# silu(c) times w_ada: one half of the rows summed on VectorE, the result turned in 32x32 blocks

## The chip, the cores and the metric

The kernel runs on one core of one Trainium2 chip. The metric is the device time of one execution in microseconds (us), the median over the runs shown. The engines are named as in the profile: PE is TensorE (PEld its weight loads), DVE is VectorE, ACT is ScalarE, POOL is GpSimd, SP is SyncE, which here only issues DMAs.

## What is computed

A decoder layer on x (512 tokens of 2048 features). Only its opening matters here:

```python
mod = silu(c) @ w_ada[l] + b_ada[l]
shift, scale, gate = split(mod, 3, axis=-1)
h = rmsnorm(x, ln_g[l]) * (1.0 + scale[:, None]) + shift[:, None]
p = h @ w_in[l] + b_in[l]
...
```

`silu(c) @ w_ada` is a product of one row of 2048 numbers with a 2048 x 6144 matrix. Its first 4096 columns (shift and scale) are needed before h exists. After p come a matrix-memory group and a sparse-attention group, an output projection, a gate, the residual and a last RMSNorm.

## The kernel before, in words

All products on float32 data are made of three single passes: an operand is split into hi + lo (`split`, line 119: ACT casts the hi half at line 123, then DVE or POOL subtracts for the lo half at line 126, as the pattern `pat` says), and PE adds hi·hi, hi·lo and lo·hi into the same PSUM bank.

The opening stage (lines 129 to 236) works on 16 k-tiles of 128 features.

- Lines 134 to 136 load the packed columns and x as four tiles xs of 128 tokens. Lines 150 to 158 take the row norms: two squares on ACT (L153), two small DVE steps (L155, L156), a power on POOL (L157), one scaling on DVE (L158).
- Lines 176 to 185 transpose x on PE (L180) into 16 tiles xt of 128 features x 512 tokens, copied out of PSUM by DVE and ACT in turn (L185, L183).
- `modulate(k)` (line 190) loads one tile of weights kow (448 KB) and, in `gemv`, the four ada tiles of this k-tile (4 x 512 KB, line 167). `gemv` multiplies them with cb, which is silu(c) repeated over 32 columns: 16 matmuls of 256 columns, four at a time in the four column groups of PE (L169), which leave four partial sums in the PSUM tile gp_s. DVE copies them out (L173), and two matmuls with one column each (L195, L196; the column sel holds ones at the four partial sums) add them and turn the result so that features lie on partitions. DVE makes the shift and the factor md from them (L198 to L200), then hf = xt·factor + shift (L202); ACT casts hf to hhi (L205); DVE subtracts for hlo (L206).
- `first_tiles(k)` (line 211) splits kow and issues 21 matmuls of 512 columns into seven PSUM tiles ko: seven of hhi with the hi half (L218), seven of hlo with the hi half (L220), seven of hhi with the lo half (L221).

The loop at line 226 calls `modulate(k + 1)` ahead of `first_tiles(k)`. The order on each engine is then chosen by the framework's scheduler; `tc.issue_after` holds an instruction behind another. Buffers that bound the overlap: eight ada tiles (two k-tiles), three kow tiles, four hi and four lo halves (two k-tiles), one PSUM bank "o" for gp_s. All DMAs go through SP in one queue. After the stage, `proj` (line 238) does the same three-pass product for the other column tiles of w_in.

Of the kernel before, what the change touches and what calls it, by code (L numbers as in the profile page):

```python
# [86 lines left out]
def layer_kernel(ctx: ExitStack, tc: tile.TileContext, x, cols, ada, ada_g, w_ko, w_tiles,  # L87
# [71 lines left out]

    lastdma = [None]  # L160

    def gemv(step, name):
        """silu(c) @ 256 columns of w_ada: four partial sums, one per quadrant of rows"""
        gpb = psb("o", f"gp_{name}")
        for kk in range(4):
            raw = ada_tile(f"ada{name}_{kk}")
            lastdma[0] = nc.sync.dma_start(raw, ada[step, kk]).ins
            for j in range(4):
                pe.matmul(gpb[32 * j:32 * j + 32, 0:256], cb[:, 4 * kk + j, :],  # L169
                          raw[:, j * 256:(j + 1) * 256], start=(kk == 0), stop=(kk == 3),  # L170
                          tile_position=(0, 32 * j))
        gv = st.tile([P, 256], F32, tag="gv", name=f"gv{name}", bufs=2)
        ve.tensor_copy(gv, gpb[:, 0:256])  # L173
        return gpb, gv

    xt = []
    for k in range(KT):
        tp = psb(("pj", "pj", "sc", "sc", "tp", "tp", "ms", "o")[k % 8], f"xt{k}")
        for i in range(NT):
            pe.transpose(tp[:, i * P:(i + 1) * P], xs[i][:, k * P:(k + 1) * P], ident)  # L180
        xt.append(hp.tile([P, T], F32, name=f"xts{k}", tag=f"hlo{k}"))
        if k % 2:
            sc.copy(xt[k], tp)  # L183
        else:
            ve.tensor_copy(xt[k], tp)  # L185
    hhi, hlo = [], []
# [3 lines left out]
    def modulate(k):  # L190
        """h^T of 128 features as hi + lo"""
        raw = raw_tile(f"kow{k}")
        nc.sync.dma_start(raw[:, :KO], w_ko[k * P:(k + 1) * P, :])
        gpb, gv = gemv(k, f"s{k}")
        pe.matmul(gpb[:, 256:257], gv[:, 0:128], col("sel"), start=True, stop=True)  # L195
        last = pe.matmul(gpb[:, 257:258], gv[:, 128:256], col("sel"), start=True, stop=True)  # L196
        md = st.tile([P, 2], F32, name=f"md{k}", tag="md", bufs=2)
        ve.tensor_add(md[:, 0:1], gpb[:, 256:257], col("b_shift", k))  # L198
        ve.tensor_scalar(md[:, 1:2], gpb[:, 257:258], col("b_scale", k), 1.0, op0=ALU.add, op1=ALU.add)
        ve.tensor_mul(md[:, 1:2], md[:, 1:2], col("ln_g", k))  # L200
        hf = st.tile([P, T], F32, name=f"hf{k}", tag="hf", bufs=2)
        ve.tensor_scalar(hf, xt[k], md[:, 1:2], md[:, 0:1], op0=ALU.mult, op1=ALU.add)  # L202
        hh = hp.tile([P, T], F32R, tag=f"hhi{k}", name=f"hhi{k}")
        hl = hp.tile([P, T], F32R, tag=f"hlo{k}", name=f"hlo{k}")
        sc.copy(hh, hf)  # L205
        ve.tensor_sub(hl, hf, hh.bitcast(F32))  # L206
        hhi.append(hh)
        hlo.append(hl)
        return raw, last.ins

    def first_tiles(k, raw, after):
        """the products of one k-tile; those beyond the first few are issued behind `after`"""
        for j0, nj in ((0, 4), (4, 3)):
            wh, wl = split(raw[:, j0 * P:(j0 + nj) * P], nj * P, f"ko{k}_{j0}")
            for j in range(nj):
                ps = ko_ps[j0 + j]
                c = slice(j * P, (j + 1) * P)
                pe.matmul(ps, wh[:, c], hhi[k], start=(k == 0), stop=False)  # L218
                with tc.issue_after(after) if after is not None and j0 + j >= JSEL else nullcontext():
                    pe.matmul(ps, wh[:, c], hlo[k], start=False, stop=False)  # L220
                    pe.matmul(ps, wl[:, c], hhi[k], start=False, stop=(k == KT - 1))  # L221
# [68 lines left out]
    def q_evac(ps, name):  # L290
        """the stacks [hi; lo] and [lo; hi] of the two heads in a tile"""
# [11 lines left out]
    # gate logits (input gates, forget gates, branch gates) as rows  # L303
# [57 lines left out]
    # gaps between tiles of tokens: gp_[h, j, i] = sum of the totals of tiles j .. i-1  # L361
# [14 lines left out]
    # tokens paired by parity on the partitions, with the position term of either block half  # L376
# [21 lines left out]
    def compress(kv):  # L398
        """keys and values of the compressed blocks"""
# [60 lines left out]
    def attend(g, qs, kh, kl, vt):  # L460
# [6 lines left out]
        for i in reversed(range(NT)):  # L467
# [522 lines left out]
```

## Time and profile before

| | us |
|---|---|
| median of 3 runs | 1149.93 (1147.37 to 1151.27) |
| span of the profiled execution, first to last instruction | 1147.1 |
| PE busy in it | 1120.0 |
| DVE busy | 646.4 |
| ACT busy | 531.3 |
| POOL busy | 198.3 |

The profiled execution is one more execution. Its span is 2.8 us below the median of the timed runs and 0.3 us below the lowest of them; what lies around the span is not listed apart. In the profile's rows a matmul's duration contains its pipeline, so two matmuls of one line can overlap; how often a new one starts is read from the start times. A row "x32" covers 32 instructions, from the first start to the last end. One float32 `pe.matmul` gives two records, one for each of two passes.

### The profile page before, as it was taken

The page shows a single profiled execution, that of the slowest core. Times are in us where ns is not written, and L with a number is a line of the kernel's source. Part 1 is how long each engine was busy: PE and PEld are TensorE (multiplying, and loading weights), DVE is VectorE, ACT ScalarE, POOL GpSimd, SP SyncE. Part 2 cuts the span into 40 slices and gives each one's busy share as a digit, 9 for nine tenths or more (in the row PEclk, how much of TensorE's full clock was granted, in tenths as well). Part 3 has the DMA queues.
Part 4 walks back from the last instruction along what each step waited for, and adds up shares of the span by engine and source line. Part 5 has one row for each costly group of instructions (what it writes and reads, how often), then busy time and mean ns, then how long its engine had stood idle before and what let it go on. Part 6 is the DMA issues. An engine that isn't in the chain of part 4 may idle for free.

```text
span 1147.1 us, 16515 instructions
## 1 busy us (share of the span) xinstructions
PE 1120.0 (98%) x5924; PEld 919.0 (80%) x5924; DVE 646.4 (56%) x1649; ACT 531.3 (46%) x1206; POOL 198.3 (17%) x174
## 2 busy tenths in 40 slices
PE   5999999999999999999999999999999999999997
PEld 4677788888888788788788778888888888888896
DVE  5444446205566656775757785668667357344273
ACT  5222253226667657756666743433433354233242
POOL 0000110333235324333533220000000001000000
PEclk9999999999999999999999999999999999999998
DMA  9999432332122122112211353238526332544334
GB/s 371 400 344 351 183 111 90 122 94 91 55 62 68 56 58 73 54 58 64 66 56 56 121 175 92 74 129 279 162 74 198 84 89 73 163 138 125 105 121 156
DMA packets 49330, 150.17 MB, mean 131 GB/s; under 512 B 5856, under 2 KB 7776, under 8 KB 48736
## 3 DMA queue, kind: packets, MB, share of 16 engines
q1 hardware_dynamic: 49248, 149.12, 39.7%
q8 instruction: 46, 0.75, 0.3%
q14 instruction: 36, 0.29, 0.1%
HBM read 144.90 MB, written 4.19 MB: 130 GB/s over the span
## 4 chain that ended last, share of the span: by engine, by line
PE 94%; DVE 3%; DMA 2%; issue 1%; ACT 1%; SPq 0%; ACTq 0%; POOLq 0%; DVEq 0%
PE po L860 4%; PE po L861 4%; PE po L862 4%; PE gp_s L169 3%; PE pj_q L250 3%; PE pj_mz L250 3%; PE pj_mx L250 3%; PE pj_mz L251 3%; PE pj_q L251 3%; PE pj_mz L252 3%; PE pj_mv L250 3%; PE pj_q L252 3%; PE pj_mx L251 3%; PE pj_mv L252 3%; PE pj_mx L252 3%; PE pj_mv L251 3%
## 5 line engine op out<-in xcount | busy, mean ns | idle before, releaser
L485 ACT ACTIVATE ep<-ep,nm 128x512 f32<-128x512 f32 (+3 forms) x128 | 71.2, 557 | 19.4 <-DVE nm L478 18.7
L710 POOL TENSOR_TENSOR sm<-sm,mhalf 128x1 f32<-128x1 f32 x16 | 10.1, 638 | 253.8 <-DVE sm L709 112.5
L749 DVE SCALAR_TENSOR_TENSOR gacc<-adag,sil,gacc 128x512 f32<-128x512 f32 x60 | 48.5, 809 | 8.9 <-DMA adag<-in_dram 8.2
L478 DVE CUSTOM_DVE_ANT_0 ep<-ss,bias 128x512 f32<-128x512 f32 (+3 forms) x64 | 30.3, 486 | 30.7 <-PE tps L504 22.1
L123 ACT CAST ko_0h<-kow 128x512 fp32r<-128x512 f32 x16 | 9.9, 620 | 76.0 <-PE ko L220 76.0
L478 DVE CUSTOM_DVE_ANT_0 ep<-sw,bias 128x512 f32<-128x512 f32 (+3 forms) x64 | 29.9, 486 | 18.9 <-PE sw L546 12.9
L498 DVE TENSOR_SCALAR ep<-ep,ff 128x512 f32<-128x512 f32 (+3 forms) x80 | 33.2, 463 | 0.6
L822 POOL TENSOR_TENSOR rf<-rf,mhalf 128x1 f32<-128x1 f32 x4 | 2.2, 547 | 178.8 <-ACT tz L815 163.1
L508 DVE TENSOR_TENSOR pls<-tps,phs 128x512 fp32r<-128x512 f32 x40 | 27.1, 685 | 10.5 <-ACT phs L507 10.1
L169 PE MATMUL gp_s<-adas,cb 128*32 128x256 f32 x512 | 31.2, 382 | 0.4 <-PE gp_s L196 0.4
L508 DVE TENSOR_TENSOR plw<-tpw,phw 128x512 fp32r<-128x512 f32 x40 | 27.3, 685 | 6.7 <-ACT phw L507 6.0
L465 POOL TENSOR_SCALAR bias<-ct 128x640 f32<-128x640 f32 x16 | 29.4, 1838 | 2.3 <-DVE nm L478 1.2
L507 ACT CAST phw<-tpw 128x512 fp32r<-128x512 f32 x40 | 22.8, 582 | 13.3 <-PE tpw L504 8.4
L485 ACT ACTIVATE ec<-ec,nm 128x32 f32<-128x32 f32 x64 | 20.3, 317 | 17.6 <-DVE nm L478 17.2
L507 ACT CAST phs<-tps 128x512 fp32r<-128x512 f32 x40 | 23.0, 581 | 11.2 <-DVE nm L478 5.0
L504 PE MATMUL tpw<-ct,ep 128*128 128x128 f32 x160 | 26.6, 272 | 0.1
L220 PE MATMUL ko<-hlo,ko_0h 128*128 128x512 f32 x64 | 26.4, 412 | 0.0
L169 PEld LDWEIGHTS gp_s<-adas,cb 128*32 128x32 f32 x512 | 15.1, 110 | 13.8 <-PE ko L220 4.9
L496 ACT ACTIVATE ep<-ep,ff 128x512 f32<-128x512 f32 (+3 forms) x48 | 23.5, 552 | 4.4 <-DVE ff L490 4.3
L478 DVE CUSTOM_DVE_ANT_0 ec<-ss,bias 128x32 f32<-128x32 f32 x48 | 9.0, 188 | 29.1 <-PE ss L536 28.8
L221 PE MATMUL ko<-hhi,ko_0l 128*128 128x512 f32 x64 | 24.9, 390 | 0.0
L504 PE MATMUL tps<-ct,ep 128*128 128x128 f32 x160 | 24.9, 272 | 0.0
(1082 smaller groups left out, 3824.0 us busy)
## 6 DMA issues: line engine op xcount, KB each, us to landing
adas<-in_dram SPq DMA_DIRECT2D x64, 512.0 KB, 7.5
adag<-in_dram SPq DMA_DIRECT2D x64, 256.0 KB, 3.8
wo<-in_dram SPq DMA_DIRECT2D x32, 512.0 KB, 3.6
w_q<-in_dram SPq DMA_DIRECT2D x16, 512.0 KB, 3.7
w_mx<-in_dram SPq DMA_DIRECT2D x16, 512.0 KB, 3.6
w_mv<-in_dram SPq DMA_DIRECT2D x16, 512.0 KB, 3.7
w_mz<-in_dram SPq DMA_DIRECT2D x16, 512.0 KB, 3.6
w_mo<-in_dram SPq DMA_DIRECT2D x16, 512.0 KB, 3.7
```

The source lines that it names most:

```text
L169: pe.matmul(gpb[32 * j:32 * j + 32, 0:256], cb[:, 4 * kk + j, :], raw[:, j * 256:(j + 1) * 256], start=(kk == 0), stop=(kk == 3), tile_pos ...
L250: pe.matmul(ps, wh[:, c], hhi[k], start=(k == 0), stop=False)
L251: pe.matmul(ps, wh[:, c], hlo[k], start=False, stop=False)
L252: pe.matmul(ps, wl[:, c], hhi[k], start=False, stop=(k == KT - 1))
L478: ve.tensor_tensor_reduce(dst, src, bs, -0.125, 3.0e38, ALU.add, ALU.min, nm[:, c:c + 1])
L485: sc.activation(tiles[hd], tiles[hd], AF.Exp, bias=nm[:, 4 * br + hd:4 * br + hd + 1], scale=-1.0, accum_out=zz[:, 4 * br + hd:4 * br + hd ...
L504: pe.transpose(tp[0:rows, hd * P:(hd + 1) * P], srcs[hd], ident)
L508: ve.tensor_sub(pl[0:rows, :], tp[0:rows, :], ph[0:rows, :].bitcast(F32))
L749: ve.scalar_tensor_tensor(acc, raw, w, acc, op0=ALU.mult, op1=ALU.add)
L860: pe.matmul(pss[i][:, :cn], yh[k][:, t], wh[:, c], start=f0, stop=False)
L861: pe.matmul(pss[i][:, :cn], yh[k][:, t], wl[:, c], start=False, stop=False)
L862: pe.matmul(pss[i][:, :cn], yl[k][:, t], wh[:, c], start=False, stop=l0)
```

## The change

Within the opening stage:

- `gemv` takes the four ada tiles of a k-tile in the order 2, 3, 0, 1. The first two are multiplied on PE, now with 64 instead of 256 columns per matmul: each of the four column groups takes its own 32 columns of shift and of scale (8 rows x 4 groups, 64 records). The other two are summed on DVE into acc: one multiplication and seven multiply-adds of 128x256. A ninth round of four matmuls with a tile of ones adds acc into the same PSUM tile.
- The copy gv and the sel matmuls go. One DVE transpose in 32x32 blocks turns the PSUM tile, and md comes from two DVE instructions instead of three (bs1 = b_scale + 1 is made once).
- ACT makes hhi from xt, factor and shift directly, beside DVE's hf, and no longer from hf.
- Both lo halves of kow are made on POOL in the whole stage (`pat[0] = "p"`).
- `first_tiles` goes over the seven tiles three times: hhi with hi, hhi with lo, hlo with hi; the third round is issued behind the ones matmuls of the next k-tile.
- All loads of the stage are chained in program order: x, ada 0, kow 0, ada 1, kow 1, and so on. One of the two squares of each x tile is made on DVE, the scaling is done in two halves, and seven transposes of x stand ahead of the first product, nine behind.

```diff
     for i in range(NT):
-        nc.sync.dma_start(xs[i], x[i * P:(i + 1) * P, :])
+        lastdma[0] = nc.sync.dma_start(xs[i], x[i * P:(i + 1) * P, :]).ins
+    ones = const.tile([P, P], F32, name="ones")
+    gp.memset(ones, 1.0)
...
-    cb = st.tile([P, KT, 32], F32, name="cb")
-    ve.tensor_copy(cb, sil.unsqueeze(2).to_broadcast([P, KT, 32]))
+    cb = st.tile([P, KT // 2, 32], F32, name="cb")
+    ve.tensor_copy(cb, sil[:, KT // 2:].unsqueeze(2).to_broadcast([P, KT // 2, 32]))
+    bs1 = st.tile([P, KT], F32, name="bs1")
+    ve.tensor_scalar_add(bs1, col("b_scale", 0, KT), 1.0)
...
-        for hf in range(2):
-            junk = ada_tile(f"junk{i}{hf}")
-            sc.activation(junk, xs[i][:, hf * 1024:(hf + 1) * 1024], AF.Square,
-                          accum_out=ss[:, 2 * i + hf:2 * i + hf + 1])
+        junk = [ada_tile(f"junk{i}{hf}") for hf in range(2)]
+        sc.activation(junk[0], xs[i][:, 0:1024], AF.Square, accum_out=ss[:, 2 * i:2 * i + 1])
+        ve.tensor_tensor_reduce(junk[1], xs[i][:, 1024:], xs[i][:, 1024:], 1.0, 0.0, ALU.mult, ALU.add,
+                                ss[:, 2 * i + 1:2 * i + 2])
...
-        ve.tensor_scalar_mul(xs[i], xs[i], rr[:, i:i + 1])
+        for hf in range(2):
+            xh = xs[i][:, hf * 1024:(hf + 1) * 1024]
+            ve.tensor_scalar_mul(xh, xh, rr[:, i:i + 1])
+
+    def load_ada(k):
+        raws = []
+        for kk in (2, 3, 0, 1):
+            raw = ada_tile(f"ada{k}_{kk}")
+            with tc.issue_after(lastdma[0]):
+                lastdma[0] = nc.sync.dma_start(raw, ada[k, kk]).ins
+            raws.append(raw)
+        raw = raw_tile(f"kow{k}")
...
+    def gemv(k, raws):
+        acc = st.tile([P, 256], F32, tag="acc", name=f"acc{k}", bufs=2)
+        for r in range(8):
+            w = raws[2 + r // 4][:, (r % 4) * 256:(r % 4 + 1) * 256]
+            if r == 0:
+                ve.tensor_scalar_mul(acc, w, sil[:, r:r + 1])
+            else:
+                ve.scalar_tensor_tensor(acc, w, sil[:, r:r + 1], acc, op0=ALU.mult, op1=ALU.add)
+        gpb = psb("o", f"gp{k}")
+        for r in range(9):
+            w = acc if r == 8 else raws[r // 4][:, (r % 4) * 256:(r % 4 + 1) * 256]
+            w = w.rearrange("p (s c) -> p s c", s=2)
+            for g in range(4):
+                c = slice(32 * g, 32 * g + 32)
+                last = pe.matmul(gpb[c, 0:64].rearrange("p (s c) -> p s c", s=2), ones[:, 0:32] if r == 8 else cb[:, r, :],
+                          w[:, :, c], start=(r == 0), stop=(r == 8), tile_position=(0, 32 * g))
+        tr = st.tile([P, 64], F32, tag="tr", name=f"tr{k}", bufs=2)
+        ve.transpose(tr, gpb[:, 0:64])
+        md = st.tile([P, 2], F32, name=f"md{k}", tag="md", bufs=2)
+        ve.tensor_add(md[:, 0:1], tr[:, 0:1], col("b_shift", k))
+        ve.tensor_scalar(md[:, 1:2], tr[:, 32:33], bs1[:, k:k + 1], col("ln_g", k), op0=ALU.add, op1=ALU.mult)
+        return md, last.ins
...
+    def modulate(k, md):
         hf = st.tile([P, T], F32, name=f"hf{k}", tag="hf", bufs=2)
-        ve.tensor_scalar(hf, xt[k], md[:, 1:2], md[:, 0:1], op0=ALU.mult, op1=ALU.add)
...
-        sc.copy(hh, hf)
+        sc.activation(hh, xt[k], AF.Identity, scale=md[:, 1:2], bias=md[:, 0:1])
+        ve.tensor_scalar(hf, xt[k], md[:, 1:2], md[:, 0:1], op0=ALU.mult, op1=ALU.add)
         ve.tensor_sub(hl, hf, hh.bitcast(F32))
...
+        w = [split(raw[:, j0 * P:(j0 + nj) * P], nj * P, f"ko{k}_{j0}") for j0, nj in ((0, 4), (4, 3))]
+        for p in range(3):
+            for j in range(NKO):
+                wh, wl = w[j // 4]
+                c = slice(j % 4 * P, (j % 4 + 1) * P)
+                with tc.issue_after(after) if p == 2 and after is not None else nullcontext():
+                    pe.matmul(ko_ps[j], (wl if p == 1 else wh)[:, c], (hlo if p == 2 else hhi)[k],
+                              start=(k == 0 and p == 0), stop=(k == KT - 1 and p == 2))
+
+    pat[0] = "p"
```

Where the change moves instructions, the order on three engines is this. The names end in a buffer number; the digit ahead of it is the k-tile.

PE, before, from the product of k-tile 7 on (gp_s7 is its PSUM tile, ko0 to ko6 the first column tiles):

```order
L169 MATMUL gp_s7_703<-adas7_3_722,cb_82 32x256 x4
L218 MATMUL ko0_232<-hhi6_668,ko6_0h_742 128x512
L220 MATMUL ko0_232<-hlo6_669,ko6_0h_742 128x512
L221 MATMUL ko0_232<-hhi6_668,ko6_0l_743 128x512
L218 MATMUL ko4_236<-hhi6_668,ko6_4h_758 128x512
L195 MATMUL gp_s7_703<-ct_67,gvs7_728 128x1
L196 MATMUL gp_s7_703<-ct_67,gvs7_728 128x1
L220 MATMUL ko2_234<-hlo6_669,ko6_0h_742 128x512
```

The same place in the changed kernel:

```order
L195 MATMUL gp7_910<-ada7_2_856,cb_86 32x64 x16
L195 MATMUL gp7_910<-ada7_3_858,cb_86 32x64 x16
L248 MATMUL ko0_317<-hhi6_896,ko6_0h_962 128x512
L248 MATMUL ko6_323<-hhi6_896,ko6_4l_967 128x512
L195 MATMUL gp7_910<-acc7_901,ones_80 32x64 x4
L248 MATMUL ko0_317<-hlo6_897,ko6_0h_962 128x512
L248 MATMUL ko6_323<-hlo6_897,ko6_4h_966 128x512
L195 MATMUL gp8_1006<-ada8_2_952,cb_86 32x64 x16
```

Only the first and the last matmul of a round on ko stand here. Ahead of the ones matmuls there are 14 matmuls on ko, behind them seven, and then the next product begins.

DVE, before, from the copy of the partial sums of k-tile 4 on (ko5_0l and ko5_4l are lo halves of kow 5):

```order
L173 COPY gvs4_518<-gp_s4_493 128x256
L198 TENSOR_TENSOR md4_522<-gp_s4_493,ct_67 128x1
L199 TENSOR_SCALAR md4_522<-gp_s4_493,ct_67 128x1
L200 TENSOR_TENSOR md4_522<-md4_522,ct_67 128x1
L202 TENSOR_SCALAR hf4_526<-xts4_153,md4_522 128x512
L126 TENSOR_TENSOR ko5_0l_673<-kow5_561,ko5_0h_672 128x512
L206 TENSOR_TENSOR hlo4_529<-hf4_526,hhi4_528 128x512
L126 TENSOR_TENSOR ko5_4l_689<-kow5_561,ko5_4h_688 128x384
```

DVE in the changed kernel, from the transpose of k-tile 5 to that of k-tile 6:

```order
L199 STREAM_TRANSPOSE tr5_755<-gp5_718 128x64
L201 TENSOR_TENSOR md5_757<-tr5_755,ct_67 128x1
L202 TENSOR_SCALAR md5_757<-tr5_755,bs1_88,ct_67 128x1
L213 TENSOR_SCALAR hf5_799<-xts5_188,md5_757 128x512
L214 TENSOR_TENSOR hlo5_801<-hf5_799,hhi5_800 128x512
L186 TENSOR_SCALAR acc6_805<-ada6_0_764,sil_84 128x256
L188 SCALAR_TENSOR_TENSOR acc6_805<-ada6_0_764,sil_84,acc6_805 128x256 x3
L188 SCALAR_TENSOR_TENSOR acc6_805<-ada6_1_766,sil_84,acc6_805 128x256 x4
L199 STREAM_TRANSPOSE tr6_851<-gp6_814 128x64
```

The two lo halves left DVE, and the eight instructions on acc stand between the hlo of one k-tile and the transpose of the next. From k-tile 4 on every step reads like this.

POOL, before, after the four powers of the row norms (rst and zt belong to the attention group):

```order
L157 TENSOR_TENSOR rr_87<-rr_87,mhalf_84 128x1 x4
L336 MEMSET rst_1534 4x512
L344 MEMSET zt_1541 64x512
```

POOL in the changed kernel, two of the 16 k-tiles that follow the powers:

```order
L126 TENSOR_TENSOR ko5_0l_867<-kow5_672,ko5_0h_866 128x512
L126 TENSOR_TENSOR ko5_4l_871<-kow5_672,ko5_4h_870 128x384
L126 TENSOR_TENSOR ko6_0l_963<-kow6_768,ko6_0h_962 128x512
L126 TENSOR_TENSOR ko6_4l_967<-kow6_768,ko6_4h_966 128x384
```

In the stage POOL was empty behind the powers; now it has two subtractions for each k-tile.

## Rows read from the trace of the kernel before

**Rows 1.** The page: busy time of PE, and the chain that ended last.
```profile
PE 1120.0 (98%) x5924; PEld 919.0 (80%) x5924; DVE 646.4 (56%) x1649; ACT 531.3 (46%) x1206; POOL 198.3 (17%) x174
...
PE 94%; DVE 3%; DMA 2%; issue 1%; ACT 1%; SPq 0%; ACTq 0%; POOLq 0%; DVEq 0%
```

**Rows 2.** Busy time by stretch: PE, PEld, DVE, ACT, POOL, clock, DMA share, GB/s.
```profile
20.00:40.00 20.00, 18.48 (x171) 13.19 (x169) 10.57 (x24) 5.55 (x11) 0.00 (x0) 1.00 1.03 408
60.00:120.00 60.00, 60.00 (x465) 43.33 (x464) 25.90 (x64) 13.23 (x24) 0.00 (x0) 1.00 0.96 350
```

**Rows 3.** Timeline, PE: one step of the stage, and step 15 (start, length).
```profile
57.25 1.93 PE L169 MATMUL gp_s<-adas,cb 128*32 128x256 f32 x32
...
60.83 0.39 PE L221 MATMUL ko<-hhi,ko_0l 128*128 128x512 f32 x1
61.06 0.84 PE L218 MATMUL ko<-hhi,ko_4h 128*128 128x512 f32 x3
...
61.74 0.28 PE L195 MATMUL gp_s<-ct,gvs 128*128 128x1 f32 x2
...
130.25 1.93 PE L169 MATMUL gp_s<-adas,cb 128*32 128x256 f32 x32
```

**Rows 4.** Timeline, PE: the first 25 ns of one product.
```profile
57.25 0.42 PE L169 MATMUL gp_s<-adas,cb 128*32 128x256 f32 x4
```

**Rows 5.** Timeline, DVE: the start, one step, and the last step of the stage.
```profile
17.26 1.28 DVE L158 TENSOR_SCALAR xs<-xs,rr 128x2048 f32<-128x2048 f32 x1
...
19.99 4.87 DVE L185 COPY xts<-xt 128x512 f32<-128x512 f32 x8
...
26.63 0.16 DVE L198 TENSOR_TENSOR md<-gp_s,ct 128x1 f32<-128x1 f32 x1 [0.70 <-PE gp_s L196]
...
62.28 0.16 DVE L198 TENSOR_TENSOR md<-gp_s,ct 128x1 f32<-128x1 f32 x1 [2.60 <-PE gp_s L196]
...
62.79 0.55 DVE L202 TENSOR_SCALAR hf<-xts,md 128x512 f32<-128x512 f32 x1
...
64.38 0.68 DVE L206 TENSOR_TENSOR hlo<-hf,hhi 128x512 fp32r<-128x512 f32 x1
...
135.28 0.16 DVE L198 TENSOR_TENSOR md<-gp_s,ct 128x1 f32<-128x1 f32 x1 [2.60 <-PE gp_s L196]
```

**Rows 6.** Groups by line and shape: busy, mean ns of one.
```profile
L169 PEld LDWEIGHTS gp_s<-adas,cb 128*32 128x32 f32 x512 | 15.1, 110 | 13.8 <-PE ko L220 4.9 <-PE gp_s L196 0.5 <-issue 0.4
...
L205 ACT CAST hhi<-hf 128x512 fp32r<-128x512 f32 x16 | 9.8, 615 | 3.9 <-DVE hf L202 3.9
L173 DVE COPY gvs<-gp_s 128x256 f32<-128x256 f32 x16 | 6.8, 425 | 16.7 <-PE gp_s L169 16.7
L498 DVE TENSOR_SCALAR ep<-ep,ff 128x256 f32<-128x256 f32 x20 | 6.0, 350 | 0.2
L388 DVE SCALAR_TENSOR_TENSOR cst<-pj_vc,ct 64x256 f32<-64x256 f32 x16 | 7.1, 480 | 6.3 <-PE pj_vc L252 6.2
```

**Rows 7.** Timeline, DVE: two chained multiply-adds on one accumulator.
```profile
764.00 1.54 DVE L589 SCALAR_TENSOR_TENSOR acc<-xp,ct,acc 128x512 f32<-128x512 f32 x2
```

**Rows 8.** One line's instructions: ns shortest/median/longest.
```profile
L749 DVE SCALAR_TENSOR_TENSOR gacc<-adag,sil,gacc x60: 731/748/1855, 649.0 to 891.6; 128x512 f32<-128x512 f32 x60
...
L126 POOL TENSOR_TENSOR w_k_00l<-w_k,w_k_00h x4: 1288/1292/1297, 205.5 to 388.1; 128x512 fp32r<-128x512 f32 x4
```

**Rows 9.** Timeline, DVE and POOL: two places where they meet in SBUF.
```profile
494.17 0.75 DVE L589 SCALAR_TENSOR_TENSOR acc<-xp,ct,acc 128x512 f32<-128x512 f32 x1
...
494.34 1.73 POOL L126 TENSOR_TENSOR w_mv_00l<-w_mv,w_mv_00h 128x512 fp32r<-128x512 f32 x1 [3.01 <-ACT w_mv_00h L123]
...
595.40 1.29 POOL L126 TENSOR_TENSOR w_mz_00l<-w_mz,w_mz_00h 128x512 fp32r<-128x512 f32 x1 [0.24 <-ACT w_mz_00h L123]
...
595.48 1.76 DVE L589 SCALAR_TENSOR_TENSOR acc<-xp,ct,acc 128x512 f32<-128x512 f32 x1
```

**Rows 10.** DMA issues of the first 140 us: size, median us to landing.
```profile
adas<-in_dram SPq DMA_DIRECT2D x64, 512.0 KB, 7.5
kow<-in_dram SPq DMA_DIRECT2D x16, 448.0 KB, 6.1
```

More of the change, by code (lines that the diff above doesn't have):

```diff
@@ L134, in layer_kernel @@
     nc.sync.dma_start(ct[:, :NEARLY], cols[:, :NEARLY])
+    lastdma = [None]
     for i in range(NT):
-        nc.sync.dma_start(xs[i], x[i * P:(i + 1) * P, :])
+        lastdma[0] = nc.sync.dma_start(xs[i], x[i * P:(i + 1) * P, :]).ins
+    ones = const.tile([P, P], F32, name="ones")
+    gp.memset(ones, 1.0)
+    mhalf = const.tile([P, 4], F32, name="mhalf")
+    gp.memset(mhalf, -0.5)
     sil = const.tile([P, KT], F32, name="sil")
     sc.activation(sil, col("c", 0, 16), AF.Silu)
-    cb = st.tile([P, KT, 32], F32, name="cb")
-    ve.tensor_copy(cb, sil.unsqueeze(2).to_broadcast([P, KT, 32]))
-    mhalf = const.tile([P, 4], F32, name="mhalf")
-    gp.memset(mhalf, -0.5)
+    cb = st.tile([P, KT // 2, 32], F32, name="cb")
+    ve.tensor_copy(cb, sil[:, KT // 2:].unsqueeze(2).to_broadcast([P, KT // 2, 32]))
+    bs1 = st.tile([P, KT], F32, name="bs1")
+    ve.tensor_scalar_add(bs1, col("b_scale", 0, KT), 1.0)
     ss = st.tile([P, 2 * NT], F32, name="ss")
@@ L157, in layer_kernel @@
         gp.tensor_tensor(rr[:, i:i + 1], rr[:, i:i + 1], mhalf[:, 0:1], op=ALU.pow)
-        ve.tensor_scalar_mul(xs[i], xs[i], rr[:, i:i + 1])
[L160 to L185, printed above, removed]
-    hhi, hlo = [], []
-    ko_names = list(TILES)[:NKO]
-    ko_ps = [psb(t, f"ko{i}") for i, t in enumerate(("pj", "pj", "sc", "sc", "tp", "tp", "ms"))]
@@ L190, in modulate @@
[L190 to L200, printed above, removed]
+        for hf in range(2):
+            xh = xs[i][:, hf * 1024:(hf + 1) * 1024]
+            ve.tensor_scalar_mul(xh, xh, rr[:, i:i + 1])
@@ new lines, in load_ada @@
+    def load_ada(k):
[6 more added lines that the diff above has]
+        raw = raw_tile(f"kow{k}")
+        with tc.issue_after(lastdma[0]):
+            lastdma[0] = nc.sync.dma_start(raw[:, :KO], w_ko[k * P:(k + 1) * P, :]).ins
+        return raws, raw
+    def gemv(k, raws):
[20 more added lines that the diff above has]
+        return md, last.ins
@@ L208, in modulate @@
         hlo.append(hl)
-        return raw, last.ins
-    def first_tiles(k, raw, after):
[L213 to L221, printed above, removed]
@@ L223, in layer_kernel, with transposes @@
-    JSEL = 2
+    xt = []
+    def transposes(ks):
+        for k in ks:
+            tp = psb(("pj", "pj", "sc", "sc", "tp", "tp", "ms")[k % 7], f"xt{k}")
+            for i in range(NT):
+                pe.transpose(tp[:, i * P:(i + 1) * P], xs[i][:, k * P:(k + 1) * P], ident)
+            xt.append(hp.tile([P, T], F32, name=f"xts{k}", tag=f"hlo{k}"))
+            if k % 2:
+                sc.copy(xt[k], tp)
+            else:
+                ve.tensor_copy(xt[k], tp)
+    raws, raw = load_ada(0)
@@ new lines, in layer_kernel @@
+    nraws, nraw = load_ada(1)
+    transposes(range(7))
+    md, _ = gemv(0, raws)
+    transposes(range(7, KT))
+    modulate(0, md)
+    ko_names = list(TILES)[:NKO]
+    ko_ps = [psb(t, f"ko{i}") for i, t in enumerate(("pj", "pj", "sc", "sc", "tp", "tp", "ms"))]
+    def first_tiles(k, raw, after):
+        w = [split(raw[:, j0 * P:(j0 + nj) * P], nj * P, f"ko{k}_{j0}") for j0, nj in ((0, 4), (4, 3))]
[6 more added lines that the diff above has]
+                              start=(k == 0 and p == 0), stop=(k == KT - 1 and p == 2))
@@ L224, in layer_kernel @@
+    pat[0] = "p"
     w2s = const.tile([P, 192], F32, name="w2s")
-    raw, _ = modulate(0)
     for k in range(KT):
-        rnext, after = modulate(k + 1) if k + 1 < KT else (None, None)
-        if k == KT - 2:
+        after = None
+        if k + 1 < KT:
+            md, after = gemv(k + 1, nraws)
+            nxt = nraw
+            if k + 2 < KT:
+                nraws, nraw = load_ada(k + 2)
+        if k == KT - 3:
             with tc.issue_after(lastdma[0]):
@@ L234, in layer_kernel @@
         first_tiles(k, raw, after)
-        raw = rnext
+        if k + 1 < KT:
+            modulate(k + 1, md)
+            raw = nxt
+    pat[0] = "v"
     stpool.__exit__(None, None, None)
@@ L324, in layer_kernel @@
     ve.tensor_copy(gt.rearrange("p a b -> p (a b)"), gps[:, :256])
-    ones = const.tile([P, P], F32, name="ones")
-    gp.memset(ones, 1.0)
     zc = const.tile([P, NT, 64], F32, name="zc")
```

## The prediction

> **What bounds the kernel now.** I read the page first: PE is busy 98% of the span and makes 94% of the chain of work that ended last [rows 1]. That is a mean over all stages, so the next view is the busy time by stretch. Between 60 and 120 us, inside the opening stage, PE is busy in all 60.00 us at the full clock, POOL does nothing, and the DMAs bring 350 GB/s, though they brought 408 between 20 and 40 us [rows 2]. So no transfer holds this stage: PE does. The timeline of PE gives the step: the product of one k-tile starts at 57.25 us, that of ten k-tiles later at 130.25, so a step is 73.00 / 10 = 7.30 us [rows 3]. Two things follow. To be faster, a step must become shorter on PE, and no other engine may need more than PE then does. And what follows the stage is bound by PE too, in an order that the change leaves alone, so what the stage gains or loses reaches the end in full. A measurement of this kernel tells about 0.3% (3.4 us) from no change.
>
> **PE's step in the change.** A matmul on ko follows the last one after 61.06 - 60.83 = 0.23 us; a single one lasts 0.39 to its end and three last 0.84, so (0.84 - 0.39) / 2 = 0.225 [rows 3]; I take 0.226. The 21 of a step take 21 x 0.226 = 4.75 us, before and after. The product now is eight rounds of four records: (1.93 - 0.42) / 7 = 0.216 us each, 1.73 in all [rows 3, 4]. Of 7.30 us, 0.82 are left for the two sel pairs and the changes between kinds of work. The changed product has 18 rounds of four records (16, and 2 with the ones), each with a quarter of the columns. The trace has no such matmul. Below: a quarter of 0.216, 0.054 a round. Above: 0.216 a round, if a matmul costs the same however few columns it has. I take 0.06, near the lower end: the four records of a round last 0.42 us together [rows 4], no longer than one ko matmul alone (0.39), so starting a record costs next to nothing and a round's pace is that of its columns. That is 18 x 0.06 = 1.08 us. With 0.7 for the changes of work (as many as before, without the sel pairs) PE's step is 4.75 + 1.08 + 0.7 = **6.5 us**; with the upper end 4.75 + 3.89 + 0.7 = 9.3. Between them lies the weight load, which takes 0.110 us a record now [rows 6]: if the loads of one column group can't overlap, 18 x 0.110 = 2.0 and a step of 7.4.
>
> [...]
>
> **DMAs.** A step still moves 4 x 512 + 448 KB [rows 10], 2.56 MB; at the 408 GB/s seen [rows 2] that takes 6.3 us. The five issues of a step stay in SP's one queue, only in another order. Covered by 6.5 us or more; if nothing else bound the step, 6.3 would be next.
>
> **DVE's loop.** This is the new wait. The ones matmuls need acc complete; the transpose needs the ones matmuls; and in DVE's order hf, hlo and the whole acc of the next k-tile stand behind that transpose, so the next ones matmuls wait for all of it. Nothing of this loop can overlap itself. Term by term:
> - From the end of acc over PE to the transpose: before, sel starts at 61.74 and DVE follows at 62.28, 0.54 us for two pairs of matmuls [rows 3, 5]; I take 0.4 for eight small records.
> - The transpose of 128x64: not in the trace. Between the 128x1 step of 0.16 us [rows 5] and the PSUM copy of 128x256, 0.425 [rows 6]; I take 0.28.
> - md in two steps: three took from 62.28 to 62.79, 0.51 us [rows 5]; two take 0.3.
> - hf, which lasts 0.55, and beside it on ACT hhi of 0.615 [rows 5, 6], with its signal to DVE 0.70; then hlo, 0.65 to 0.68 [rows 5]: 1.35 together. Before, hhi stood behind hf; this gain lies on the loop and is counted by this.
> - acc: the multiplication of 128x256 takes 0.350, the multiply-add 0.480 on 64 partitions [rows 6], and in a chain on one accumulator two of 512 columns last 1.54 [rows 7], 0.04 to 0.06 more than two single ones of 0.748 [rows 8]. So (0.35 + 0.04) + 7 x (0.48 + 0.04) = 4.03 us.
>
> That is 0.4 + 0.28 + 0.3 + 1.35 + 4.03 = 6.36 us, just below PE's 6.5.
>
> **POOL beside it.** The two lo halves go from DVE to POOL. One of 128x512 takes 1.29 us there [rows 8], one of 128x384 by that about 0.97, together 2.26 a step: far under 7.3, so POOL as an engine bounds nothing. But where it meets DVE, one waits for the other. At 595.40 POOL starts a subtraction, at 595.48 DVE a multiply-add; POOL ends at 596.69 and DVE's takes 1.76 us where its like takes 0.75. At 494.17 DVE is first and POOL's takes 1.73 in place of 1.29 [rows 9]. The 60 multiply-adds of line 749 have a median of 748 ns and a longest of 1855 [rows 8]. So a DVE instruction on two SBUF operands and a POOL subtraction don't run together. DVE then loses up to 2.26 us a step, and nothing where POOL works during the PSUM wait, the transpose, md or hf. When does POOL get its input? ACT's cast of kow stands behind hhi in ACT's order, so the first hi half is there as DVE begins hlo, and then DVE has five microseconds of two-operand work. I take 1.0 (the measured loss) for the first half and 0.65 for the second, part of which falls past the end of acc: 1.65. Loop: 6.36 + 1.65 = **8.0 us**, between 6.36 and 8.6.
>
> **The start.** Before, md of k-tile 0 comes at 26.63 us [rows 5]. In the change DVE makes, after the scaling (which ends about where it did, 18.54 [rows 5]; squares and scalings only trade places between ACT and DVE), the same eight copies of xt, 4.87 us from 19.99 on [rows 5], and between them the eight steps of acc 0, 4.03, and the first of acc 1, 0.39; then the transpose, 0.28. 19.99 + 4.87 + 4.03 + 0.39 + 0.28 = 29.6, so the first md is 2.9 us later (between 0.5, if acc fills DVE's waits, and 4, if POOL cuts in). In return the first loop has one step of acc less, -0.4.
>
> **Sum.** Before, 15 intervals from md 0 (26.63) to md 15 (135.28 [rows 5]) are 108.65 us, 7.24 each. After: 15 x (8.0 - 7.24) = +11.4. Behind the last md stand 28 matmuls on ko instead of 31, 3 x 0.226 = -0.7. Edits at nothing: bs1 and the smaller cb (made while x loads), the ones tile (POOL, idle there), the x transposes' order (PE waits for ada 0 there). 2.9 + 11.4 - 0.4 - 0.7 = +13.2. Against the profiled execution that is a span of 1147.1 + 13.2 = 1160.3; its span is 2.8 below the median of the runs, so I add to the median: 1149.93 + 13.2 = **1163.1 us**. With a loop of 8.6 it is 1172, with 7.6 it is 1157.
>
> **Rivals.**
> - *PE stays the bound.* POOL's work finds DVE's gaps, or waits without delaying it, and the step is 6.5 us: 2.9 + 15 x (6.5 - 7.24) - 0.7 = -8.9, **1141 us**, faster. For it: DVE alone needs only 6.36. Against it: the meetings of [rows 9], and five microseconds of two-operand work in a row. The kernel is faster as long as DVE loses less than about 0.5 us a step (a step under 6.9). 0.20.
> - *Half the meeting is avoided.* If ACT casts kow early, one half fits the 1.0 us of wait, transpose and md. Then some 0.65 is lost, a loop of 7.0: -3.6 + 2.9 - 0.4 - 0.7 = -1.8, **1148 us**, no change. 0.13.
> - *PE pays by the record.* Rounds of 0.216 whatever their columns, a step of 9.3: 15 x 2.06 + 2.9 - 0.7 = +33, **1183 us**, slower still. Against it: [rows 4]. 0.07.
> - *The opening alone.* The reordered loads and transposes bring md 0 no later, with any of these steps: 2 to 3 us less. Inside the ranges.
>
> [...]
>
> **How the numbers follow.** DVE's loop as the bound, with a loss to POOL of about 1.65 us a step: 0.55, its own range 1156 to 1172 (loops of 7.55 to 8.6). The rivals 0.20, 0.13 and 0.07; 0.05 for what I have not seen, split over both sides. The range of all: it takes in the forecast, the no-change case and most of the faster one, and leaves out the 0.07 and the faster tail: 1139 to 1175. Faster by over 0.3%: 0.20 + 0.03 = 0.23. Within 0.3%: 0.12. Slower: 0.65.
>
> **What would show it.** Right: the products of two k-tiles start 8.0 us apart on PE; PE idles some 1.5 us a step ahead of the ones matmuls (line 195), released by DVE's acc; the multiply-adds of line 188 have a mean well over 0.48, a few of them 1.2 to 1.5; POOL's 128x512 take 1.3 to 1.9. Wrong: products 6.3 to 6.8 us apart and PE without that wait (first rival); multiply-adds and hlo not lengthened (second); rounds of line 195 that start 0.2 us apart (third); md 0 before 28 us (the start).

## The result: 1.1% slower, and the profile after

The changed kernel takes 1162.52 us (median of 4 runs, 1160.65 to 1163.44), the kernel before 1149.31 on the same chip: a ratio of 1.0113 with a 95% interval of 1.0097 to 1.0129. The forecast was 1163.1.

The page of the changed kernel, busy times and the chain that ended last (against [rows 1]):

```profile
PE 1117.4 (96%) x6500; PEld 921.5 (79%) x6500; DVE 712.1 (61%) x1742; ACT 529.8 (46%) x1198; POOL 237.9 (21%) x206
...
PE 87%; DVE 9%; ACT 2%; DMA 1%; issue 1%; POOL 0%; SPq 0%; ACTq 0%; POOLq 0%; DVEq 0%
```

PE works less (1117.4 us instead of 1120.0) and the span is longer (1159.9 instead of 1147.1). On the chain DVE rises from 3% to 9%: that is the place to look. One step of the stage, timeline of DVE (start, length; the bracket is the idle time before and its releaser), and what POOL does beside it:

```profile
75.49 0.25 DVE L199 STREAM_TRANSPOSE tr<-gp 128x64 f32<-128x64 f32 x1 [0.44 <-PE gp L195]
75.78 0.16 DVE L201 TENSOR_TENSOR md<-tr,ct 128x1 f32<-128x1 f32 x1
75.85 0.27 DVE L202 TENSOR_SCALAR md<-tr,bs,ct 128x1 f32<-128x1 f32 x1
76.16 0.55 DVE L213 TENSOR_SCALAR hf<-xts,md 128x512 f32<-128x512 f32 x1
77.00 0.69 DVE L214 TENSOR_TENSOR hlo<-hf,hhi 128x512 fp32r<-128x512 f32 x1 [0.30 <-ACT hhi L212]
77.61 1.38 DVE L186 TENSOR_SCALAR acc<-ada,sil 128x256 f32<-128x256 f32 x1
79.03 4.24 DVE L188 SCALAR_TENSOR_TENSOR acc<-ada,sil,acc 128x256 f32<-128x256 f32 x7
83.71 0.25 DVE L199 STREAM_TRANSPOSE tr<-gp 128x64 f32<-128x64 f32 x1 [0.44 <-PE gp L195]
```

```profile
77.56 1.28 POOL L126 TENSOR_TENSOR ko_0l<-kow,ko_0h 128x512 fp32r<-128x512 f32 x1 [5.91 <-ACT ko_0h L123]
78.80 1.07 POOL L126 TENSOR_TENSOR ko_4l<-kow,ko_4h 128x384 fp32r<-128x384 f32 x1
```

From transpose to transpose 83.71 - 75.49 = 8.22 us pass, and DVE has only two short waits in them: the loop is its work and its waits on PE and ACT. The first step on acc lasts 1.38 us while POOL's subtraction runs beside it. PE in the same step:

```profile
77.18 1.10 PE L195 MATMUL gp<-ada,cb 128*32 128x64 f32 x64
78.21 1.19 PE L248 MATMUL ko<-hhi,ko_0h 128*128 128x512 f32 x4
...
80.84 0.84 PE L248 MATMUL ko<-hhi,ko_4l 128*128 128x512 f32 x3
83.33 0.32 PE L195 MATMUL gp<-acc,ones 128*32 128x64 f32 x8 [1.65 <-DVE acc L188]
```

PE stands still for 1.65 us ahead of the ones matmuls, released by DVE's acc. Ten of the steps have such a wait, 14.9 us in all; between 60 and 120 us of the kernel before there was none [rows 2].

### The profile page after: what moved, and what is told of

It is laid out like the page before. It is cut to its first block, busy times and chain, and to the rows that moved or that the text cites. A ratio compares the mean times of both kernels' runs of the same rounds, so it can differ in the third digit from the quotient of the medians.

```text
span 1159.9 us, 17799 instructions
## 1 busy us (share of the span) xinstructions
PE 1117.4 (96%) x6500; PEld 921.5 (79%) x6500; DVE 712.1 (61%) x1742; ACT 529.8 (46%) x1198; POOL 237.9 (21%) x206
## 4 chain that ended last, share of the span: by engine, by line
PE 87%; DVE 9%; ACT 2%; DMA 1%; issue 1%; POOL 0%; SPq 0%; ACTq 0%; POOLq 0%; DVEq 0%
DVE acc L188 5%; PE po L893 4%; PE po L895 4%; PE po L894 4%; PE pj_q L285 3%; PE pj_mx L285 3%; PE pj_mo L287 3%; PE pj_q L286 3%; PE pj_mv L285 3%; PE pj_q L287 3%; PE pj_mz L285 3%; PE pj_mx L286 3%; PE pj_mv L287 3%; PE pj_mz L286 3%; PE pj_mx L287 3%; PE pj_mv L286 3%
## 5 line engine op out<-in xcount | busy, mean ns | idle before, releaser
L188 DVE SCALAR_TENSOR_TENSOR acc<-ada,sil,acc 128x256 f32<-128x256 f32 x112 | 69.6, 622 | 3.5
L212 ACT ACTIVATE hhi<-xts,md 128x512 fp32r<-128x512 f32 x16 | 13.1, 817 | 94.1 <-DVE md L202 94.1
L126 POOL TENSOR_TENSOR ko_0l<-kow,ko_0h 128x512 fp32r<-128x512 f32 x16 | 21.1, 1318 | 88.7 <-ACT ko_0h L123 88.7
L195 PEld LDWEIGHTS gp<-ada,cb 128*32 128x32 f32 x1024 | 18.7, 128 | 8.1 <-issue 4.3
L224 PE MATMUL xt<-ct,xs 128*128 128x128 f32 x64 | 10.6, 325 | 14.5 <-DVE xs L165 13.6
```

Source lines behind the costliest of these rows:

```text
L188: ve.scalar_tensor_tensor(acc, w, sil[:, r:r + 1], acc, op0=ALU.mult, op1=ALU.add)
```

## Experiments

Unless said otherwise each kernel is the change with one edit. The kernel before, timed beside them on the same chips, had medians of 1150.4, 1149.8, 1150.5 and 1148.9 us in the four groups.

**Is it POOL? The lo halves made once.**

```diff
-        lo = ws.tile([P, 512], F32R, tag="wlo", name=name + "l", bufs=4)
         sc.copy(hi[:, :n], raw)
+        if keep in los:
+            return hi, los[keep]
...
+            lo = los[keep] = st.tile([P, 512], F32R, tag=f"lok{keep}", name=name + "l", bufs=1)
```

> The lo halves of w_ko are made for k-tile 0 only and used for all 16 (15 of 16 left out): POOL does nothing in the stage, DVE's own work and PE's are as in the change. If DVE's loop bounds the step and POOL's subtractions lengthen it, the loop falls from 8.2 us by the two losses seen in the trace (1.03 at line 186, 0.64 over the seven multiply-adds) to 6.5 to 6.7 and the kernel to about 1142 us. If the meeting with POOL is not what costs (the chain on acc is slow by itself, or the loads), the step stays near 8 us and the time within 4 us of 1162.

1141.1 us, ratio to before 0.9923 (0.9908 to 0.9938). A step takes 6.56 us, and the same two rows of DVE are now:

```profile
104.72 0.35 DVE L193 TENSOR_SCALAR acc<-ada,sil 128x256 f32<-128x256 f32 x1
105.10 3.61 DVE L195 SCALAR_TENSOR_TENSOR acc<-ada,sil,acc 128x256 f32<-128x256 f32 x7
109.15 0.25 DVE L206 STREAM_TRANSPOSE tr<-gp 128x64 f32<-128x64 f32 x1 [0.44 <-PE gp L202]
```

1.38 falls to 0.35 and 4.24 to 3.61, together 1.66 us: that is the whole difference between 8.22 and 6.56. PE has no wait left (busy in all 60.00 us from 60 to 120), but DVE's loop is just as long, 6.56: neither has room to spare. This kernel leaves out work, the lo halves of 15 k-tiles; without POOL beside DVE the same split of the product would beat the kernel before.

**Both lo halves back on DVE.**

```diff
-    pat[0] = "p"
+    pat[0] = "v"
```

> Both lo halves on DVE, as before the change, all else as in the change. DVE then has no partner to wait for but 0.65 + 0.55 us more of its own: 6.5 + 1.2 = 7.7 us a step, about 1156 us. If moving them to POOL had really freed DVE, this would be slower than the change, 1170 or more.

1143.5 us, ratio 0.9945 (0.993 to 0.9959): far below the 1156 I expected. The steps are 6.49 us early in the stage, where DVE waits for PE, and 6.73 and 6.99 in turn later. Part of one late step on DVE:

```profile
104.52 0.27 DVE L202 TENSOR_SCALAR md<-tr,bs,ct 128x1 f32<-128x1 f32 x1
104.70 0.34 DVE L186 TENSOR_SCALAR acc<-ada,sil 128x256 f32<-128x256 f32 x1
104.96 0.55 DVE L213 TENSOR_SCALAR hf<-xts,md 128x512 f32<-128x512 f32 x1
105.42 0.48 DVE L188 SCALAR_TENSOR_TENSOR acc<-ada,sil,acc 128x256 f32<-128x256 f32 x1
105.81 0.69 DVE L214 TENSOR_TENSOR hlo<-hf,hhi 128x512 fp32r<-128x512 f32 x1
106.41 2.05 DVE L188 SCALAR_TENSOR_TENSOR acc<-ada,sil,acc 128x256 f32<-128x256 f32 x4
```

The scheduler put other work between dependent steps, and that work is nearly free: hlo no longer waits 0.30 us for hhi, and a multiply-add with another instruction behind it lets that start 0.39 us later (105.42 to 105.81), where one in a chain takes 3.61 / 7 = 0.515. My 1.2 us for the two lo halves was added to a loop with holes, and most of it fell into them: the late steps are 6.86 on the mean, 0.3 more than without lo halves.

**Is 0.515 the chain? Two accumulators in turn.**

```diff
-        acc = st.tile([P, 256], F32, tag="acc", name=f"acc{k}", bufs=2)
+        accs = [st.tile([P, 256], F32, tag=f"acc{i}", name=f"acc{k}_{i}", bufs=2) for i in range(2)]
         for r in range(8):
+            acc = accs[r % 2]
...
-        for r in range(9):
+        for r in range(10):
```

> The eight rows on DVE go into two accumulators in turn, and the ones round is doubled; POOL still makes the lo halves. Multiply-adds that follow one another on one accumulator start 0.515 us apart, one that follows an unrelated copy 0.39. If the chain itself costs 0.11 us a link, the loop loses 6 x 0.11 and gains 0.13 for two more rounds: 8.2 to 7.6 us, 1153 us, lower if the first steps fill the wait for hhi. If 0.515 is what a multiply-add costs anyway, the time is 1162 to 1165.

1147.8 us, ratio 0.9987 (0.9978 to 0.9997); the late steps take 7.34.

```profile
94.26 2.40 DVE L187 TENSOR_SCALAR acc<-ada,sil 128x256 f32<-128x256 f32 x2
96.58 2.45 DVE L189 SCALAR_TENSOR_TENSOR acc<-ada,sil,acc 128x256 f32<-128x256 f32 x6
```

Six multiply-adds in 2.45 us, 0.41 each: a link of the chain costs some 0.11 us, as expected. Both meetings with POOL now sit in the two multiplications. The time is 5 us below the 1153 expected: a late step loses 0.88 us, not some 0.6, for the second multiplication is shorter than the multiply-add it replaces (0.35 against 0.48 us, each without POOL beside it), and DVE waits no longer than before, 0.44 us, for the doubled ones matmuls.

**Place or amount? POOL with one half only.**

```diff
-    pat[0] = "p"
+    pat[0] = "vp"
```

> POOL makes only the 512-column lo half, DVE the one of 384. If each subtraction on POOL costs DVE nearly its whole length, this keeps the loss of 1.03 us and trades 0.64 for 0.47 of DVE's own: a step of about 7.5 to 7.9, between lo all on DVE (1143.5 us) and lo all on POOL (1162.5): about 1154 to 1159. If one subtraction is absorbed in DVE's waits, 1146 or less.

1155.1 us, ratio 1.0051 (1.0034 to 1.0069); steps of 7.55 and 7.93 in turn, as forecast.

```profile
98.16 1.38 DVE L186 TENSOR_SCALAR acc<-ada,sil 128x256 f32<-128x256 f32 x1
99.57 3.09 DVE L188 SCALAR_TENSOR_TENSOR acc<-ada,sil,acc 128x256 f32<-128x256 f32 x6
...
105.10 0.35 DVE L186 TENSOR_SCALAR acc<-ada,sil 128x256 f32<-128x256 f32 x1
105.49 0.69 DVE L214 TENSOR_TENSOR hlo<-hf,hhi 128x512 fp32r<-128x512 f32 x1
106.10 1.51 DVE L188 SCALAR_TENSOR_TENSOR acc<-ada,sil,acc 128x256 f32<-128x256 f32 x1
```

In both steps one instruction pays about 1.03 us: the multiplication in one (1.38 instead of 0.35, started at 98.16 us with POOL at 98.10), a multiply-add in the next (1.51 instead of 0.48).

**POOL held behind acc, first try.** The subtraction was put under `issue_after` of the last multiply-add, once with both halves and once with the 512 half alone, and the hi halves of kow got six buffers of their own.

```diff
-        eng.tensor_sub(lo[:, :n], raw, hi[:, :n].bitcast(F32))
+        with tc.issue_after(hold) if hold is not None and eng is gp else nullcontext():
+            eng.tensor_sub(lo[:, :n], raw, hi[:, :n].bitcast(F32))
```

> Both lo halves stay on POOL, but each pair is held behind the last multiply-add of acc, so that the first subtraction runs while DVE waits for the ones matmuls and the transpose (0.44 + 0.25 us) instead of at the start of acc. If the place decides, the first costs DVE some 0.4 us instead of 1.03 and the second, which then meets hf and hlo, 0.6 to 0.7: a step of 7.5 instead of 8.2, about 1152 us. If POOL's length is paid wherever it falls, 1162.

> The same with only the 512-column half on POOL, held behind the last multiply-add, and that of 384 on DVE. Against the same split without the hold (1155.1 us, steps of 7.5 to 7.9): if the place decides, 0.6 of the 1.03 us go, steps of 6.9 to 7.3, 1145 to 1147 us. If the length is paid anywhere, 1155.

1163.8 us (ratio 1.012, 1.0103 to 1.0137) and 1155.2 (1.0043, 1.0028 to 1.0058): the times without the edit. They say nothing of the place, because POOL hadn't moved:

```profile
103.16 1.43 DVE L193 TENSOR_SCALAR acc<-ada,sil 128x256 f32<-128x256 f32 x1
...
103.16 1.28 POOL L128 TENSOR_TENSOR ko_0l<-kow,ko_0h 128x512 fp32r<-128x512 f32 x1 [5.97 <-ACT ko_0h L124]
```

POOL starts as ACT's cast is done, with acc just begun. Between these two engines `issue_after` put no wait on the chip here; what the two runs are good for is that they repeat the two times above.

**POOL held behind acc by a real dependency.** DVE writes one column of each lo tile from the finished acc, so POOL must wait for it. The hi halves have their six buffers here too, which alone changed nothing in the first try.

```diff
+        if hold is not None and eng is gp:
+            ve.tensor_copy(lo[:, 0:1], hold[:, 0:1])
         eng.tensor_sub(lo[:, :n], raw, hi[:, :n].bitcast(F32))
```

> The same idea with a real wait: DVE writes one column of each lo tile from acc behind the last multiply-add (two small steps in the wait for the ones matmuls), so POOL can't start a pair of subtractions before acc is done. All else is the change. If the place decides, the first subtraction falls into the ones wait and the transpose, where DVE works from PSUM or not at all, and costs some 0.4 us instead of 1.03; the second meets hf, hlo and costs 0.6 to 0.7: 7.5 us a step, 1152 us. If POOL's length is paid wherever it falls, 8.2 and 1162; over 1165 if the lo halves now come late for PE.

1156.2 us, ratio 1.0062 (1.0045 to 1.0078): steps of 7.73.

```profile
88.42 0.25 DVE L208 STREAM_TRANSPOSE tr<-gp 128x64 f32<-128x64 f32 x1
88.70 1.08 DVE L210 TENSOR_TENSOR md<-tr,ct 128x1 f32<-128x1 f32 x1
...
90.00 1.01 DVE L222 TENSOR_SCALAR hf<-xts,md 128x512 f32<-128x512 f32 x1
91.12 0.69 DVE L223 TENSOR_TENSOR hlo<-hf,hhi 128x512 fp32r<-128x512 f32 x1
91.73 0.35 DVE L194 TENSOR_SCALAR acc<-ada,sil 128x256 f32<-128x256 f32 x1
92.11 3.61 DVE L196 SCALAR_TENSOR_TENSOR acc<-ada,sil,acc 128x256 f32<-128x256 f32 x7
95.83 0.15 DVE L128 CAST ko_0l<-acc 128x1 fp32r<-128x1 f32 x1
```

```profile
88.46 1.30 POOL L129 TENSOR_TENSOR ko_0l<-kow,ko_0h 128x512 fp32r<-128x512 f32 x1 [5.48 <-PE gp L204]
89.72 1.01 POOL L129 TENSOR_TENSOR ko_4l<-kow,ko_4h 128x384 fp32r<-128x384 f32 x1
```

acc is undisturbed (0.35 and 3.61), and so is the transpose from PSUM, though POOL starts beside it (88.46 and 88.42). But md's 128x1 sum takes 1.08 us instead of 0.16 and hf 1.01 instead of 0.55; hlo, which no longer has to wait for hhi, keeps its 0.69. From k-tile 3 on all steps but one read like this; in that one (104.30) POOL starts 0.4 us behind the transpose, and hf and hlo take 1.30 and 1.31. Of the 1.66 us a step some 0.5 is saved, less than the 0.7 I expected, because POOL starts only as the transpose does and then meets the very steps on which PE waits. The place matters, but most of the length is paid in this order too.

**Less for DVE: five rows instead of eight.**

```diff
+    def RV(k):
+        return 5
```

RV(k) is the number of rows that DVE sums for k-tile k. Rows 5 to 7 go to PE behind rows 8 to 15.

> Five rows of the product on DVE instead of eight, eleven on PE. DVE's loop: 8.2 - 3 x 0.52 = 6.65 us; PE's step: 6.5 + 3 x 0.135 = 6.9. If the loop is the sum of its terms, the bound goes back to PE at 6.9 us: 1162.5 - 15 x 1.1 - 1.5 (shorter first acc) = 1144 us, faster than both kernels. If the losses to POOL grow or PE's records cost more, 7.3 us or more a step and over 1150.

1140.0 us, ratio 0.9914 (0.99 to 0.9929), below both kernels and 4 us below the 1144 expected. Busy time by stretch (columns as in [rows 2]), and PE in one step:

```profile
60.00:95.00 35.00, 35.00 (x599) 28.48 (x598) 24.77 (x55) 9.91 (x17) 11.35 (x10) 1.00 1.02 399
```

```profile
63.18 1.44 PE L201 MATMUL gp<-ada,cb 128*32 128x64 f32 x88
64.43 0.29 PE L201 MATMUL gp<-acc,ones 128*32 128x64 f32 x8
64.66 1.20 PE L254 MATMUL ko<-hhi,ko_0h 128*128 128x512 f32 x4
...
69.64 1.44 PE L201 MATMUL gp<-ada,cb 128*32 128x64 f32 x88
```

PE is busy in all 35.00 us, though POOL still works beside DVE (11.35): DVE has room for the meetings. The products start 69.64 - 63.18 = 6.46 us apart from 43.80 to 95.48 us, and 6.85 after that (102.28, and two steps later 115.98). Only the late steps are the 6.9 of the sum. In the others acc is ready early, the ones matmuls stand right behind the product, and PE changes between kinds of work once less. The DMAs are at 399 GB/s, next in line, as the sum had it.

**Nothing for DVE: all rows on PE.** Sixteen rows of 64 columns, no acc, no ones.

> All 16 rows of the product on PE in the narrow form (64 columns), no acc and no ones; transpose, md and the rest as in the change. If a round of four records costs by its columns (0.065 to 0.07 us in the change's trace) the product takes 2.1 us, PE's step is 4.75 + 2.1 + 0.4 = 7.3 and bounds: 1147 to 1150 us. If a record has a price of its own that hides behind DVE's loop now, the step is 8 or more and the time over 1160.

1151.0 us, ratio 1.0012 (1.0002 to 1.0022).

```profile
103.69 1.99 PE L201 MATMUL gp<-ada,cb 128*32 128x64 f32 x128
105.62 1.20 PE L254 MATMUL ko<-hhi,ko_0h 128*128 128x512 f32 x4
...
132.07 1.77 PE L201 MATMUL gp<-ada,cb 128*32 128x64 f32 x112
134.63 0.43 PE L201 MATMUL gp<-ada,cb 128*32 128x64 f32 x16 [0.78 <-issue]
```

The 128 records are through in 1.99 us, the 32 wide ones in 1.93 [rows 3], and an undisturbed step takes 6.91 where I had 7.3. But five of fifteen steps take 7.6 to 11 us, and the mean is 7.46: that the time comes near the 1147 to 1150 of the sum is luck. In eight places PE stops with nothing to wait for that the profile shows, "issue", 6.8 us in all; in the kernel before PE stops only once behind 30 us, for 0.5 us, and that on DVE. The program has 7396 matmul records instead of 5924. Why PE stops no run shows; that the code arrives too late is a guess of mine. The queue that the profile calls "q8 instruction" brings 19 packets, 0.31 MB in all, between 20 and 145 us here, 12 (0.20 MB) in the change and 8 (0.13 MB) in the kernel before.

**The start alone.** All rows of k-tile 0 on PE, eight on DVE from k-tile 1 on.

```diff
+    def RV(k):
+        return 8 if k else 0
```

> Only the start is undone: k-tile 0's whole product on PE, so DVE makes no acc 0 between the copies of xt. By the sum of the prediction the start has 4.0 us of DVE in series that go: the first md moves from 29.9 to about 24 us and the kernel gains 3 to 4 us, 1159. If PE or x bound the start, nothing.

1157.1 us, ratio 1.0066 (1.0049 to 1.0083): 5.4 us better than the change, more than the 3 to 4 expected. The first transpose comes at 24.17 us instead of 29.42.

**What the runs add up to.** Lo halves and seven rows on DVE, k-tile 0 on PE; then with three rows of k-tile 0 on DVE.

> A version made of what the runs showed: lo halves on DVE, seven rows on DVE instead of eight, k-tile 0 all on PE. PE's step 6.5 + 0.13 = 6.63, DVE's loop 6.75 - 0.5 = 6.25: PE bounds again, and the start gains 3 us: 1136 to 1138 us, below all others. If the added PE records are paid with waits for code, 1140 or more.

> The version with lo halves and seven rows on DVE, with three rows of k-tile 0 on DVE instead of none. PE is the bound from about 22 us on and loses 4 records a row to DVE: 5 rounds fewer and 2 more for the ones, 0.2 us; if DVE's three steps fit its waits between the copies of xt, 1139 to 1140 us, the same as with none; if the first md comes later by them, 1141 to 1142.

1139.7 us (ratio 0.9915, 0.9897 to 0.9933) and 1140.5 (0.9926, 0.9912 to 0.9941), no clear difference. The first misses its 1136 to 1138, though the step is what was forecast, 6.63 to 6.67:

```profile
85.00:105.00 20.00, 20.00 (x304) 14.98 (x303) 17.66 (x43) 5.22 (x9) 0.00 (x0) 1.00 1.00 375
```

PE never waits, POOL is empty. What is missing lies at the start: md 0 comes 5 us earlier than in the change, but the first three intervals take 22.4 us instead of 3 x 6.65 = 20.0 (the first alone 10.03: PE then has the transposes of x and the whole product to do), so about half of the gain stays. Three versions, this one, the one with five rows and the one without POOL's work, end within 1.5 us of one another. With PE full and the DMAs at 375 to 399 GB/s I expect no split of these rows to give much more; that is not shown.

## Why the prediction was right

**The bound.** The forecast was that DVE's loop through acc, not PE, sets the step. It does: transposes are 8.2 us apart from the fifth interval on, PE waits up to 1.73 us a step for acc (1.5 was forecast), and taking POOL's work away or rows off DVE leaves PE without a wait.

**The loop, term by term.** Predicted, then measured in the step shown: ones matmuls to transpose 0.4, 0.44; transpose 0.28, 0.29 to the next start; md 0.3, 0.38; hf to the end of hlo 1.35, 1.45 (hhi from two per-partition operands takes 0.817 us on ACT, not the 0.615 of a cast, and DVE waits 0.30 for it); acc alone 4.03, 0.38 + 3.61 = 3.99 in the run without POOL's work; POOL 1.65, 1.66. The sum is 8.22 where I had 8.0. The mean over all 15 intervals is 8.00, because the first ones were shorter (6.76, 7.17, 7.84, 7.84): there the order on DVE has steps on acc between md and hlo, which the sum had not seen. So the right 8.0 is two misses of opposite sign.

**POOL.** The loss of 1.0 us was taken from one meeting in another stage [rows 9], and it held (1.03). The 0.65 of the second half came out (0.64), but not for my reason: I let part of that half fall past the end of acc, and POOL is through at 79.87 us, long before acc at 83.27. What was too narrow is the condition: I spoke of instructions with two SBUF operands, and took hf and md for safe, which no row showed. The multiplication of line 186 reads one tensor and pays 1.03 us, and in the run with the dependency hf (1.01 us instead of 0.55) and even md's 128x1 sum (1.08 instead of 0.16) take longer.

**PE's step.** 6.5 us was right: 6.49 in the early steps of the run with the lo halves on DVE, where DVE waits for PE, and 6.56 in the run without lo halves, where the two are about equal. Rounds of four narrow records cost (78.21 - 77.18) / 16 = 0.064 us where I took 0.06, so the rival of a price by the record falls. The 64 records, each 219 ns long by the profile's median, follow one another at 1.03 us / 64 = 16 ns, in four column groups.

**The start and the tail.** md 0 was forecast at 29.6 us; it comes at 29.94. The last md step starts at 149.66, 14.4 us later than before [rows 5], and the span is 12.8 longer: the tail gives back 1.6 us, where I had 0.7. In the run without POOL's work the same stretch is 2.8 us shorter than before; why it is more than the three matmuls of the sum, no run shows. Put together, the span grew by 3.3 + 11.1 - 1.6 = 12.8 us, where the sum had 2.9 + 11.4 - 0.4 - 0.7 = 13.2.

**The rivals.** That PE stays the bound (1141 us) is close to what happens once POOL's work is gone, 1141.1, though DVE's loop is then as long as PE's step. That half the meeting is avoided (1148) would need POOL's work moved into DVE's waits; the scheduler's order didn't do it from k-tile 4 on, and the run that forced it saved 0.5 us of the 1.66.

## What to carry to other kernels

Before moving work to a slower engine (a 128x512 subtraction takes 1.28 us on POOL, 0.69 on DVE), list what the bounding loop does at the moment that work becomes ready: two subtractions on an idle POOL cost DVE 1.66 us a step and the kernel 21 us (1162.5 against 1141.1), and on DVE itself they cost 2.4 (1143.5). Add an operation's time to a loop only where the loop has no holes; in this chain of dependent steps 1.2 us of independent work cost 0.3 a step. And when work is split between two engines, balance the split by the loop that comes out: five rows instead of eight turned +1.1% into -0.9%.

## What the hardware showed that was not expected

- DVE instructions that work from SBUF took longer where they started beside a POOL subtraction. In the change the multiplication of line 186, started 0.05 us behind a subtraction of 1.28 us, takes 1.38 us instead of 0.35, 1.03 more; with one half on POOL a multiply-add takes 1.51 instead of 0.48; in the run with the dependency hf takes 1.01 instead of 0.55 and a sum of 128x1 1.08 instead of 0.16. The transpose from PSUM does not (0.25 beside POOL and without it), nor do the copies of xt, which read PSUM too (0.68 with and without POOL). What holds the one kind and not the other, no run shows.
- Dependent multiply-adds of 128x256 start 0.515 us apart (seven in 3.61 us, lo halves made once); two chains in turn bring one every 0.41 (six in 2.45), and an unrelated instruction starts 0.39 behind one (lo halves on DVE).
- PE's granted clock was lower behind some of its new waits. Three stretches of the changed kernel (columns as in [rows 2]):

```profile
83.30:85.70 2.40, 2.37 (x15) 1.44 (x15) 1.61 (x5) 1.32 (x2) 0.00 (x0) 0.85 0.83 278
85.70:87.60 1.90, 1.90 (x65) 1.70 (x64) 1.86 (x3) 0.51 (x2) 1.82 (x2) 0.50 0.82 316
...
149.20:153.40 4.20, 4.20 (x19) 3.32 (x12) 3.03 (x7) 2.05 (x3) 1.64 (x4) 0.59 0.00 0
```

After the wait of 1.65 us the granted clock is 0.50, and the 64 narrow records take 1.94 us instead of 1.10; behind the wait of 1.73 us that ends at 99.81 us it is 1.00. Inside the stage DVE's loop covers this: the next ones matmuls, at 91.52 us, have no wait. At its end it doesn't: from 149.24 to 153.47 us eleven matmuls on ko take 4.23 us at a clock of 0.59, where the same eleven take 2.70 in the run with one half on POOL (142.41 to 145.11 us). PE is busy throughout, so some 1.5 us of this execution lie there; what they are worth in the timed runs, no run shows.
